# Four instead of two head tiles on the first half of the tokens at four phase borders, their low parts on GpSimd

## The chip, the cores and the metric

One core of one Trainium2 chip runs one program. The metric is the device time of one execution in microseconds (us). The engines in the texts: TensorE (PE), VectorE (DVE), ScalarE (ACT), GpSimd (POOL), SyncE (SP), and the DMA queues.

## What is computed

512 tokens of 1024 features pass through a first block of two layers (each a mixer and a feed-forward network, FFN, with layer norms after them) and a second block (a hybrid mixer and a mixture of experts). All is float32.

```python
def first_block(x, ...):
    for l in range(DEPTH):                       # DEPTH = 2
        ...
        x = layer_norm(ALPHA * x + m, ln1_g[l], ln1_b[l])
        f = conv_ffn(x, w_up[l], conv_w[l], conv_b[l], w_down[l])
        x = layer_norm(ALPHA * x + f, ln2_g[l], ln2_b[l])

def conv_ffn(x, w_up, conv_w, conv_b, w_down):
    h = x @ w_up
    hp = jnp.pad(h, ((0, 0), (CONV_W - 1, 0), (0, 0)))
    h = sum(hp[:, j:j + S] * conv_w[j] for j in range(CONV_W)) + conv_b
    u, g = jnp.split(h, 2, axis=-1)
    return (jax.nn.silu(g) * u) @ w_down

def odd_mixer(x, w_in, w_out, lq1, lk1, lq2, lk2, sub_g, rel_bias, layer):
    q, k, v = jnp.split(x @ w_in, 3, axis=-1)
    ...
    lam = (jnp.exp(jnp.sum(lq1 * lk1)) - jnp.exp(jnp.sum(lq2 * lk2)) + lam_init)
    o = diff_attention(q, k, v, lam, rel_bias)
    ...

def hybrid_mixer(h, w_in, b_in, ...):
    z = h @ w_in + b_in
    conv_a, conv_gate, q, k, v, o, i_pre, f_pre = jnp.split(z, ...)
    u = conv_a * jax.nn.sigmoid(conv_gate)
    u = causal_depthwise_conv(u, conv_w, conv_b)
    ...
```

## The kernel before

**Matmuls.** A float32 product is made of three matmuls: every operand is split into a high part (hi: a rounded copy made on ACT, the casts of L139, L280, L327) and a low part (lo: the rest, a subtraction on DVE or GpSimd, L140, L281, L329). `mm3` (L148 to L151) issues hi x hi, hi x lo and lo x hi. `fm_tile` computes 128 features for all 512 tokens (8 steps of 128 inputs, 24 matmuls of 128x512, or of 128x256 for half the tokens); `tm_tile` computes 128 tokens for 512 features.

**Weights.** `Stream` (L36 to L70) loads 232 units of 512 KB in a fixed order, two raw buffers deep, splits each into `wh` (ACT, L139) and `wl` (L140), with four buffers of each, and hands them out with `take(ahead)`, which also splits the next `ahead` units. The lo is a DVE subtraction, except for "easy" units, where GpSimd makes it: a range of late units, and the first NH units at each of the four heads in HEADS, (36, 102, 134, 200). NH is 3.

**Phase borders.** A phase ends with an output projection in `proj_ln` (L202). Its last part goes through the four blocks of 128 tokens one after the other; after each, `ln_finish` (L252) does the layer norm on DVE (L258 to L264; before the mixer another norm, L742 to L744, follows), and `to_fm` (L270) transposes the block on PE in two groups of four (L277, into `tp` banks of the tag `at`), with the hi copy on ACT (L280) and the lo on DVE (L281) into `xTh` and `xTl`. The transposes of blocks 0 and 1 are called inside `proj_ln`; those of blocks 2 and 3 are handed to the next phase as `pend`.

**The head of a phase.** At four borders (FFN of layer 0, mixer of layer 1, FFN of layer 1, mixer of the second block) `head_pair` (L175) starts the next phase with two tiles, 256 tokens first: 48 matmuls of 128x256, then `pend`, then the second 256 tokens. PSUM has eight banks: 2 of tag `mm`, 5 of `at`, 1 of `y`. The two head tiles take `at` banks. After it, tiles are 512 tokens wide in `mm` banks.

**Layer 1.** After the head, `stacks` and `lam` (L573) prepare the attention: lambda comes from a DMA on GpSimd's queue (L577, `wt<-in_lam_dram`), a DVE multiply (L579) and reduction (L581), an exponential on ACT (L582, with its table load) and two small DVE steps. `rel_table` (L549) sends the bias table `relo` to `reld` (L565) and spreads it with eight DMAs `skew<-reld` (L569), on the same queue. `qk(h)` turns a q tile and a k tile into stacks of hi and lo (`stack_q` L320, L321; `stack_k` L327 to L329), which the score matmuls (`ds`, L605) read. The order is `qk(0)`, `vproj(0)` (four value units, 96 matmuls of 128x512), `qk(1)`, `qk(2)`, `vproj(1)`.

**Mixer of the second block.** The head's two tiles are `conv_a` and `conv_gate` of the first 128 channels, used by `ag(0)` (L973 sigmoid, L976 product u). u feeds a convolution of 31 products on DVE, ACT and GpSimd (L754 to L766). `if_gates` (L801) projects the gates (24 matmuls, `gi`) and scans them on DVE and ACT (L816 to L825) into R, which PE transposes (`gt`, L830).

A scheduler sets the order of each engine's instructions from its own plan of times; the engines then run in that order and wait for one another through semaphores.

Of the kernel before, what the change touches and what calls it, by code (L numbers as in the profile page):

```python
# [75 lines left out]

class Kern:
    PRE, POST, FEW, LEAD = 2, 9, 2, 2
    YC, NH = 2, 3
    NPL, EASY, HEADS = 6, (200, 228), (36, 102, 134, 200)  # L80

    def __init__(self, tc, A, out, stop=None):
# [89 lines left out]
            if kt in self.steps:  # L172
                self.step()

    def head_pair(self, xT, pend):  # L175

        w0 = self.ws.take()
        w1 = self.ws.take()
        p0, p1 = self.ps("at"), self.ps("at")
        for p, w in ((p0, w0), (p1, w1)):  # L180
            self.fm_tile(p, w, xT, False, 0, 256)
        for f in pend:
            f()
        for p, w in ((p0, w0), (p1, w1)):
            self.fm_tile(p, w, xT, False, 256, 512)
        return p0, p1

    def rstd_(self, out, var, eps, scale=1.0):

# [472 lines left out]
    def layer1(self, xT, pend):  # L662
        nc, tc, A = self.nc, self.tc, self.A
        lam_init = 0.8 - 0.6 * math.exp(-0.3)
        first = self.head_pair(xT, pend)
        with self.pool("m1") as mp:
            self.mp = mp
            qks = self.stacks(2)
# [14 lines left out]
            def qk(h):  # L683
                for l in heads:
                    self.room(l, 1)
                if h == 0:
                    p, p2 = first
                else:
                    p = self.ps("mm")
                    self.fm_tile(p, self.ws.take(), xT)  # L690
                while h > 1 and ("scores", h - 2) not in self.ready:
                    self.step()
                self.stack_q(p, qks[h % 2], -0.125)
                if h:
                    p2 = self.ps("mm")
                    self.fm_tile(p2, self.ws.take(), xT)
                self.stack_k(p2, qks[h % 2])
                heads[h % 2].append(self.diff(h, qks[h % 2]))
                if h:
                    self.step()  # L700
# [9 lines left out]
                    self.step()  # L710

            qk(0)
            vproj(0)
            qk(1)
            qk(2)
            vproj(1)
            for h in range(3, 8):
# [7 lines left out]
            pend = self.out_proj()  # L725
# [190 lines left out]

    def mixer2(self, xT, pend):
        nc, tc, A = self.nc, self.tc, self.A
        first = self.head_pair(xT, pend)
        self.act2 = self.pool("act2", "left")  # L920
        ap = self.ap = self.act2.__enter__()
        mp = self.mp = self.open("m2")
# [38 lines left out]
        vec = self.vec  # L961

        def ag(j):
            if j == 0:
                pa, pg = first
            else:
                pa = self.ps("mm")
                self.fm_tile(pa, self.ws.take(), xT)
                self.step()
                pg = self.ps("at")  # L970
                self.fm_tile(pg, self.ws.take(), xT)
            s = mp.tile([128, 516], F32, name="sig", tag="z", bufs=1)[:, 0:512]
            nc.scalar.activation(s, pg, AF.Sigmoid, bias=vec[:, 1, j:j + 1])  # L973
            u = mp.tile([128, 544], F32, name="u31", tag="u31", bufs=3)
            nc.gpsimd.memset(u[:, 0:30], 0.0)
            nc.vector.scalar_tensor_tensor(u[:, 30:542], pa, vec[:, 0, j:j + 1], s, op0=ALU.add, op1=ALU.mult)  # L976
            convs.append(self.conv31(j, u))
            self.step()
# [603 lines left out]

    def ffn(self, l, xT, pend, finish_of):
        nc, tc = self.nc, self.tc
        first = self.head_pair(xT, pend)
        with self.pool("ffn") as fp:
            act = fp.tile([128, NP, 512], F32, name="act")
            cw = self.cw
# [8 lines left out]
                return h  # L1597

            for j in range(NP):
                if j == 0:  # L1600
                    pu, pg = first
                    u = conv(pu, j, "u")
                else:
                    pu = self.ps("mm")
                    self.fm_tile(pu, self.ws.take(), xT)
                    u = conv(pu, j, "u")
# [80 lines left out]
def layout(I):  # L1687
# [36 lines left out]
    f = fm(w)  # L1724
    q, k = f[:8], f[8:16]
    v = [list(vm(w[:, 2048:2560])), list(vm(w[:, 2560:3072]))]
    u += [q[0], k[0]] + v[0] + [q[1], k[1], q[2], k[2]] + v[1]
    for h in range(3, 8):
        u += [q[h], k[h]]
    u += list(dm(I["w_out_odd"][0]))  # L1730
# [75 lines left out]
```

## Time and profile before

| | us |
|---|---|
| median of the runs | 2063.57 |
| lowest and highest of them | 2062.98, 2067.83 |
| the profiled execution | 2058.57 |
| its span | 2056.9 |

In the profile's page PE is busy for 91% of the span, DVE for 46%, ACT for 37% and GpSimd for 16%. TensorE's granted clock is 0.959 of full speed (2.4 GHz) in the mean; where PE stood still it falls to 0.50. A row of the timeline has a start, a duration, the engine, the line of the program, the operation, what it writes and reads, and in brackets how long the engine stood idle before it and what released it. Matmuls are pipelined: the step from one start to the next is the cost of one, not its duration. The borders lie at about 287 us (FFN of layer 0), 660 (mixer of layer 1), 915 (FFN of layer 1) and 1290 (mixer of the second block).

### The profile page before, as it was taken

Reading aid. Unit: us, or ns where it says so; the run is one execution under the profiler, and the core shown is the slowest. Engines: PE = TensorE matmul, PEld = TensorE weight load, DVE = VectorE, ACT = ScalarE, POOL = GpSimd, SP = SyncE. Lnnn points to the kernel's source line nnn. Section 1 sums busy time; section 2 is a strip of 40 time slices with the busy share of each in tenths; the row PEclk is TensorE's granted clock in tenths of the full one; section 3 lists DMA queues with packets and bytes.
Section 4 is the critical chain, followed back from the end, with each engine's and each line's share of the span. In section 5 each row is a group of like instructions: output and inputs, shape, how many; then the busy total and the mean of one; then the engine's idle time right before and its main releaser. Section 6 shows DMA issues by size and latency. Waiting matters only on the chain. (4 is left out here: it accounts for less than half of the span.)

```text
span 2056.9 us, 28841 instructions
## 1 busy us (share of the span) xinstructions
PE 1867.7 (91%) x11078; PEld 1432.0 (70%) x11082; DVE 949.7 (46%) x1700; ACT 764.3 (37%) x1198; POOL 336.6 (16%) x344
## 2 busy tenths in 40 slices
PE   8999999999999999989999999799796698888881
PEld 6777878888887788878888888677575354444440
DVE  5556365545436456665454435766746011101113
ACT  6547334333322477724333323454731100000002
POOL 0001111111001100011111100545212112222212
PEclk9999999999999999999999999899797799999996
DMA  5221233332322513123323232322166999999994
GB/s 183 87 82 47 88 105 103 99 97 95 100 93 82 162 59 106 47 79 116 103 93 102 93 100 66 96 66 88 42 255 233 365 409 379 391 383 414 406 410 179
DMA packets 71527, 334.19 MB, mean 162 GB/s; under 512 B 10794, under 2 KB 11018, under 8 KB 49328
## 3 DMA queue, kind: packets, MB, share of 16 engines
q1 hardware_dynamic: 62784, 310.06, 41.3%
q0 software_dynamic: 7984, 17.48, 2.5%
q10 hardware_dynamic: 576, 4.19, 0.5%
q8 instruction: 116, 1.90, 0.4%
q14 instruction: 67, 0.55, 0.1%
HBM read 348.44 MB, written 14.18 MB: 176 GB/s over the span
## 5 line engine op out<-in xcount | busy, mean ns | idle before, releaser
L149 PE MATMUL mm<-xTh,wh 128*128 128x512 f32 x1000 | 394.8, 395 | 6.1 <-ACT xTh L1643 6.1
L150 PE MATMUL mm<-xTl,wh 128*128 128x512 f32 x1000 | 391.7, 392 | 0.5 <-DVE xTl L1644 0.5
L151 PE MATMUL mm<-xTh,wl 128*128 128x512 f32 x1000 | 392.0, 392 | 0.0
L140 DVE TENSOR_TENSOR wl<-wraw,wh 128x1024 fp32r<-128x1024 f32 x195 | 240.4, 1233 | 326.2 <-ACT wh L139 325.1
L139 ACT CAST wh<-wraw 128x1024 fp32r<-128x1024 f32 x232 | 243.6, 1050 | 343.8 <-PE mm L150 205.4
L1354 PE MATMUL mm<-ring,xt 128*32 128x256 f32 (+1 forms) x2432 | 195.0, 414 | 63.6 <-PEq L1451 29.9
L149 PEld LDWEIGHTS mm<-xTh,wh 128*128 128x128 f32 x1000 | 188.8, 189 | 46.0 <-ACT xTh L1643 6.1
L150 PEld LDWEIGHTS mm<-xTl,wh 128*128 128x128 f32 x1000 | 188.8, 189 | 39.8 <-DVE xTl L1644 1.1
L151 PEld LDWEIGHTS mm<-xTh,wl 128*128 128x128 f32 x1000 | 188.6, 189 | 39.4 <-issue 0.4
L1354 PEld LDWEIGHTS mm<-ring,xt 128*32 128x32 f32 (+1 forms) x2432 | 118.4, 126 | 136.1 <-issue 65.2
L140 POOL TENSOR_TENSOR wl<-wraw,wh 128x1024 fp32r<-128x1024 f32 x37 | 93.4, 2532 | 578.9 <-ACT wh L139 435.9
L1358 DVE TENSOR_TENSOR a<-a,mm 128x128 f32<-128x128 f32 x56 | 16.2, 289 | 318.8 <-ACT a L1357 307.8
L1611 POOL TENSOR_TENSOR act<-u,g 128x512 f32<-128x512 f32 x44 | 57.0, 1295 | 432.7 <-ACT g L1610 432.7
L1357 ACT ACTIVATE a<-mm 128x128 f32<-128x128 f32 x56 | 15.6, 278 | 263.2 <-PE mm L1354 258.7
L1373 PE MATMUL dn<-ring,aT 128*32 128x256 f32 (+1 forms) x1120 | 105.8, 425 | 0.8 <-DVE aT L1364 0.8
L140 DVE TENSOR_TENSOR jitl<-act,jith 128x512 fp32r<-128x512 f32 x44 | 30.5, 692 | 131.8 <-ACT jith L139 131.8
L149 PE MATMUL at<-wh,jith 128*128 128x512 f32 x220 | 85.8, 390 | 0.0
L151 PE MATMUL at<-wh,jitl 128*128 128x512 f32 x220 | 85.6, 389 | 0.0
L150 PE MATMUL at<-wl,jith 128*128 128x512 f32 x220 | 85.6, 389 | 0.0
L1378 POOL DMA_INDIRECT yd<-yo,yi x42 | 42.7, 1017 | 259.6 <-POOLq L1451 171.3
L139 ACT CAST jith<-act 128x512 fp32r<-128x512 f32 x44 | 27.4, 623 | 137.3 <-PE y L150 126.1
L150 PE MATMUL mm<-wl,xTh 128*128 128x512 f32 x192 | 76.2, 397 | 1.8 <-POOL wl L140 1.8
(467 smaller groups left out, 3257.0 us busy)
## 6 DMA issues: line engine op xcount, KB each, us to landing
ring<-in_wgu_dram SPq DMA_DIRECT2D x126, 1024.0 KB
wraw<-in_w_dram SPq DMA_DIRECT2D x232, 512.0 KB
ring<-in_wdn_dram SPq DMA_DIRECT2D x62, 1024.0 KB
gb<-in_ln_dram POOLq DMA_DIRECT2D x8, 512.0 KB, 6.7
yt<-yd ACTq DMA_DIRECT2D x4, 1024.0 KB
skew<-reld POOLq DMA_DIRECT2D x8, 320.0 KB, 9.5
x<-in_xT_dram SPq DMA_DIRECT2D x8, 256.0 KB
x<-in_x_dram SPq DMA_DIRECT2D x4, 512.0 KB
```

The lines of the kernel that those rows point to most:

```text
L139: nc.scalar.copy(h, src)
L140: (nc.gpsimd if spare else nc.vector).tensor_tensor(l, src, h.bitcast(F32), op=ALU.subtract)
L149: mm(out, lh, rh, start=first, stop=False)
L150: mm(out, lh, rl, start=False, stop=False)
L151: mm(out, ll, rh, start=False, stop=last)
L1354: mm(p[g * W:g * W + W, 0:256], xt[:, kt % n, kt // n, :], w[:, kt % 4, g * C + c:g * C + c + 256], start=kt == 0, stop=kt == KT - 1)
L1357: nc.scalar.activation(a, p[:, 0:128], AF.Silu)
L1358: V.tensor_tensor(a, a, p[:, 128:256], op=ALU.mult)
L1373: mm(p[g * W:g * W + W, 0:C], aTs[kt % n][:, (kt // n) * W:(kt // n) * W + W], w[:, kt, g * C:g * C + C], start=kt == 0, stop=kt == 3)
L1378: st = nc.gpsimd.indirect_dma_start(out=yv[G == 2], out_offset=bass.IndirectOffsetOnAxis(ap=ix, axis=0), in_=y, in_offset=None, bounds_che ...
L1611: nc.gpsimd.tensor_tensor(act[:, j, :], u, g, op=ALU.mult)
```

## The change

`head` takes the place of `head_pair`: four tiles, in the banks `mm`, `mm`, `at`, `at`, take four units, do their first 256 tokens (96 matmuls of 128x256), then the pending transposes, then the second 256 tokens. NH becomes 4, so GpSimd makes the low parts of all four (units 39, 105 and 137 come from DVE; unit 203 was GpSimd's). The phases take the second pair of tiles from the head too: the FFN its second u and g, layer 1 the q and k of its second head (so `qk(1)` stands ahead of `vproj(0)`, and the units are loaded in that order), the mixer the second pair of `conv_a` and `conv_gate`.

```diff
-    YC, NH = 2, 3
+    YC, NH = 2, 4
...
-    def head_pair(self, xT, pend):
-
-        w0 = self.ws.take()
-        w1 = self.ws.take()
-        p0, p1 = self.ps("at"), self.ps("at")
-        for p, w in ((p0, w0), (p1, w1)):
+    def head(self, xT, pend):
+
+        ts = [(self.ps(tag), self.ws.take(int(i < 3))) for i, tag in enumerate(("mm", "mm", "at", "at"))]
+        for p, w in ts:
             self.fm_tile(p, w, xT, False, 0, 256)
         for f in pend:
             f()
-        for p, w in ((p0, w0), (p1, w1)):
+        for p, w in ts:
             self.fm_tile(p, w, xT, False, 256, 512)
-        return p0, p1
+        return [p for p, _ in ts]
...
-                if h == 0:
-                    p, p2 = first
+                if h < 2:
+                    p, p2 = first[2 * h:2 * h + 2]
...
-                if h:
+                if h > 1:
                     p2 = self.ps("mm")
                     self.fm_tile(p2, self.ws.take(), xT)
...
             qk(0)
+            qk(1)
             vproj(0)
-            qk(1)
             qk(2)
...
-            if j == 0:
-                pa, pg = first
+            if j < 2:
+                pa, pg = first[2 * j:2 * j + 2]
...
-                if j == 0:
-                    pu, pg = first
+                if j < 2:
+                    pu, pg = first[2 * j:2 * j + 2]
...
-    u += [q[0], k[0]] + v[0] + [q[1], k[1], q[2], k[2]] + v[1]
+    u += [q[0], k[0], q[1], k[1]] + v[0] + [q[2], k[2]] + v[1]
```

Line numbers beyond L184 are two lower in the changed kernel (L277 becomes L275).

PE at the first FFN's border, from the last matmuls on the first token half over the transposes (`tp`) of blocks 2 and 3 to the second half. Before:

```order
L150 MATMUL at<-xTl,wh 128x256
L151 MATMUL at<-xTh,wl 128x256
L277 MATMUL tp<-ident,x 128x128 x12
L149 MATMUL at<-xTh,wh 128x256 x2
L149 MATMUL mm<-xTh,wh 128x512 x2
L150 MATMUL at<-xTl,wh 128x256
```

And now:

```order
L151 MATMUL at<-xTh,wl 128x256
L275 MATMUL tp<-ident,x 128x128 x16
L149 MATMUL mm<-xTh,wh 128x256 x2
L149 MATMUL at<-xTh,wh 128x256 x2
L150 MATMUL mm<-xTl,wh 128x256
L151 MATMUL mm<-xTh,wl 128x256
```

Four of the 16 transposes stood ahead of the first halves before; now all stand between the halves, and the two 512-wide matmuls that followed them are gone.

DVE at the start of layer 1's mixer, from the last lo of the tokens (L281, then L279) over lambda's steps (`wt`, `lams`) to the stacks `q` and `k`. Before:

```order
L281 TENSOR_TENSOR xTl<-tp,xTh 128x4x128 x3
L140 TENSOR_TENSOR wl<-wraw,wh 128x1024
L321 SCALAR_TENSOR_TENSOR q_4788<-at,q_4788 64x512
L140 TENSOR_TENSOR wl<-wraw,wh 128x1024
L321 SCALAR_TENSOR_TENSOR q_4791<-at,q_4791 64x512
L579 TENSOR_TENSOR wt<-wt 128x128
L673 TENSOR_SCALAR lams<-lams 128x1
L329 TENSOR_TENSOR k_4790<-at,k_4789 64x512
```

And now:

```order
L279 TENSOR_TENSOR xTl<-tp,xTh 128x4x128 x4
L577 TENSOR_TENSOR wt<-wt 128x128
L579 TENSOR_REDUCE lams<-wt 128x2
L671 TENSOR_SCALAR lams<-lams 128x1
L581 TENSOR_TENSOR lams<-lams 128x1
L582 TENSOR_SCALAR lams<-lams 128x1
L319 SCALAR_TENSOR_TENSOR q_4940<-mm,q_4940 64x512
L140 TENSOR_TENSOR wl<-wraw,wh 128x1024
L319 SCALAR_TENSOR_TENSOR q_4943<-mm,q_4943 64x512
L327 TENSOR_TENSOR k_4942<-mm,k_4941 64x512
```

Lambda's five steps moved ahead of both q stacks and of the value units' low parts.

GpSimd at the same border, where the low parts of the head's units stand ahead of the DMAs. Before:

```order
L1611 TENSOR_TENSOR act<-u,g 128x512 x22
L140 TENSOR_TENSOR wl<-wraw,wh 128x1024 x3
L565 DMA reld<-relo 8x640
L569 DMA skew<-reld 128x640 x8
L313 MEMSET k_4790 64x512
```

And now:

```order
L1609 TENSOR_TENSOR act<-u,g 128x512 x22
L140 TENSOR_TENSOR wl<-wraw,wh 128x1024 x4
L563 DMA reld<-relo 8x640
L567 DMA skew<-reld 128x640 x8
L311 MEMSET k_4942 64x512
```

The fourth subtraction stands ahead of `reld`, the skew DMAs and lambda's DMA behind them.

## Rows read from the trace of the kernel before

**Rows 1.** The page: busy time (share) xinstructions; GpSimd's low parts, xcount | busy, mean ns.
```profile
PE 1867.7 (91%) x11078; PEld 1432.0 (70%) x11082; DVE 949.7 (46%) x1700; ACT 764.3 (37%) x1198; POOL 336.6 (16%) x344
...
L140 POOL TENSOR_TENSOR wl<-wraw,wh 128x1024 fp32r<-128x1024 f32 x37 | 93.4, 2532 | 578.9 <-ACT wh L139 435.9
```

**Rows 2.** Timeline of PE, first FFN's border: start, us, engine, line, operation [idle before].
```profile
283.73 0.39 PE L150 MATMUL y<-wl,acth 128*128 128x512 f32 x1
...
286.67 0.40 PE L151 MATMUL y<-wh,actl 128*128 128x512 f32 x1
...
292.82 0.58 PE L150 MATMUL at<-xTl,wh 128*128 128x256 f32 x1 [1.13 <-DVE xTl L281]
...
301.00 1.47 PE L277 MATMUL tp<-ident,x 128*128 128x128 f32 x12
...
303.60 0.39 PE L150 MATMUL at<-xTl,wh 128*128 128x256 f32 x1
303.82 0.28 PE L151 MATMUL at<-xTh,wl 128*128 128x256 f32 x1
...
307.78 0.28 PE L149 MATMUL at<-xTh,wh 128*128 128x256 f32 x1
```

**Rows 3.** Timeline of DVE, first FFN's border.
```profile
292.09 0.68 DVE L281 TENSOR_TENSOR xTl<-tp,xTh 128x512 fp32r<-128x512 f32 x1
...
297.00 1.28 DVE L264 SCALAR_TENSOR_TENSOR x<-x,mv,gb 128x1024 f32<-128x1024 f32 x1
```

**Rows 4.** Windows, first FFN's border: us, busy of each engine, PEclk, DMA share, GB/s.
```profile
296.00:298.00 2.00, 2.00 (x11) 2.00 (x11) 2.00 (x2) 0.00 (x0) 0.00 (x0) 0.50 0.93 281
```

**Rows 5.** Timeline of PE, second FFN's border.
```profile
927.30 1.47 PE L277 MATMUL tp<-ident,x 128*128 128x128 f32 x12
...
929.90 0.38 PE L150 MATMUL at<-xTl,wh 128*128 128x256 f32 x1
```

**Rows 6.** Timeline of PE, the mixer's border.
```profile
1301.42 1.47 PE L277 MATMUL tp<-ident,hn 128*128 128x128 f32 x12
1303.42 0.66 PE L277 MATMUL tp<-ident,hn 128*128 128x128 f32 x4 [0.53 <-DVE xTl L281]
...
1304.62 0.39 PE L150 MATMUL at<-xTl,wh 128*128 128x256 f32 x1
```

**Rows 7.** Timeline of GpSimd, layer 1's border.
```profile
663.12 2.37 POOL L140 TENSOR_TENSOR wl<-wraw,wh 128x1024 fp32r<-128x1024 f32 x1 [1.34 <-ACT wh L139]
666.88 0.53 POOL L565 DMA_DIRECT2D reld<-relo  x1 [1.39 <-ACT relo L563]
...
676.24 0.58 POOL L577 DMA_DIRECT2D wt<-in_lam_dram  x1 [0.29 <-DMA skew<-reld]
```

**Rows 8.** Timeline of DVE, layer 1's border.
```profile
663.20 3.37 DVE L263 SCALAR_TENSOR_TENSOR x<-x,mv,gb 128x1024 f32<-128x1024 f32 x1
...
682.15 0.69 DVE L321 SCALAR_TENSOR_TENSOR q<-at,q 64x512 fp32r<-64x512 f32 x1
686.59 0.29 DVE L579 TENSOR_TENSOR wt<-wt 128x128 f32<-128x128 f32 x1 [3.75 <-DMA wt<-in_lam_dram]
```

**Rows 9.** Timeline of PE, layer 1, end of the head and the second score.
```profile
679.69 0.40 PE L149 MATMUL mm<-wh,xTh 128*128 128x512 f32 x1
...
688.16 0.76 PE L605 MATMUL ds<-k,q 128*128 128x512 f32 x1 [3.55 <-DVE k L329]
...
691.27 0.39 PE L149 MATMUL mm<-wh,xTh 128*128 128x512 f32 x1
```

**Rows 10.** Timeline of ACT, layer 1's border.
```profile
665.29 1.04 ACT L139 CAST wh<-wraw 128x1024 fp32r<-128x1024 f32 x1 [1.29 <-DMA wraw<-in_w_dram]
...
679.82 1.05 ACT L139 CAST wh<-wraw 128x1024 fp32r<-128x1024 f32 x1 [1.22 <-issue]
680.89 0.60 ACT L320 ACTIVATE q<-at 64x512 fp32r<-64x512 f32 x1
681.51 0.58 ACT L327 CAST k<-at 64x512 fp32r<-64x512 f32 x1
```

**Rows 11.** Timeline of PE, the mixer: the transposes of R.
```profile
1333.23 0.23 PE L830 MATMUL gt<-ident,R 4*128 4x4 f32 x1 [5.23 <-DVE R L823]
```

More of the change, by code (lines that the diff above doesn't have):

```diff
@@ L664, in layer1 @@
         lam_init = 0.8 - 0.6 * math.exp(-0.3)
-        first = self.head_pair(xT, pend)
+        first = self.head(xT, pend)
         with self.pool("m1") as mp:
@@ L918, in mixer2 @@
         nc, tc, A = self.nc, self.tc, self.A
-        first = self.head_pair(xT, pend)
+        first = self.head(xT, pend)
         self.act2 = self.pool("act2", "left")
@@ L1584, in ffn @@
         nc, tc = self.nc, self.tc
-        first = self.head_pair(xT, pend)
+        first = self.head(xT, pend)
         with self.pool("ffn") as fp:
```

## The prediction

> **What bounds the kernel now.** I read the page first: TensorE (PE) is busy for 91% of the span, and GpSimd makes 37 low parts of weights at 2.53 us each [rows 1]. So the time falls only where PE stands still or repeats work, and rises with every matmul that is added. I then read the PE timeline at the four phase borders that the change touches (into the first FFN, into layer 1, into the second FFN, into the mixer), since elsewhere the order of PE's instructions is the same in both kernels or only shifted; then DVE, ACT, GpSimd and the waits in the same stretches. I use "hi" and "lo" for the two parts of a split number.
>
> At the first FFN's border [rows 2] the last projection matmul starts at 286.67. The first head matmul that needs xTl starts at 292.82, after the lo of block 1 at 292.09 [rows 3]. PE then runs the 48 first halves, until 301.00, without a stop. The point for this change is what happens there: the last layer norm step of block 3 ended on DVE at 297.00 + 1.28 = 298.3 [rows 3], so the transposes of blocks 2 and 3 start at 301.00 with their input lying ready for 2.7 us. **PE does not wait for the second half of the tokens in the kernel before.** What is left is a gap of 2.6 us for 12 transposes and their evictions, until the first lo matmul of the second half at 303.60. The second FFN has the same picture: transposes at 927.30, lo matmul at 929.90 [rows 5]. The mixer's border has it with 16 transposes, the last four behind an `at` buffer (0.53 us of wait): 1301.42 to 1304.62, 3.2 us [rows 6]. Before the first xTl matmul the chain is projection, layer norm, transpose, lo, and nothing of the change is in it: on DVE the order up to the lo of block 1 is unchanged.
>
> The first stretch of head matmuls runs at half clock, 1.2 GHz, in the kernel before (granted 0.50 from 296 to 298) [rows 4]. A column costs the same there whichever tile it belongs to, so I count the half clock as equal.
>
> **The change part by part.**
>
> *More narrow matmuls.* From the rows, 33 steps of 256 columns take 307.78 - 303.82 = 3.96 us, 0.12 each, and 13 steps of 512 columns 286.67 - 283.73 = 2.94 us, 0.2265 each [rows 2]. At each border 96 more matmuls of 256 take the place of 48 of 512: 96 x 0.12 - 48 x 0.2265 = 11.52 - 10.87 = +0.65 us.
>
> *Transposes in one block.* All 16 now stand together behind the 96 first halves, with two `at` banks held by the head, which is the mixer's pattern before: 3.2 us instead of 2.6. The two FFN borders pay +0.6 each, with the 0.65 **+1.25 each, +2.5 for both**. The bounds: 0.65 if the four extra transposes find a hole, 1.9 if the last four wait twice as long.
>
> *Fourth low part on GpSimd.* Three units move from DVE to GpSimd. At the FFN borders that delays nothing that PE waits for: tile 3 of the head is used some 10 us after its hi part exists, and block 3's layer norm has over 10 us more than before. At the layer-1 border GpSimd also issues the DMAs of the bias table and of lambda. In the kernel before it finishes its third low part at 663.12 + 2.37 = 665.5, waits for `relo`, issues `reld` at 666.88, then eight skew DMAs, and lambda's at 676.24 [rows 7]. The fourth low part stands ahead of `reld`; its cast ends about 666.3 (in the kernel before that cast starts at 665.29 and takes 1.04 [rows 10]), so `reld` goes about 2 us later, at 668.9, and everything behind it on that queue too. Lambda's data, used at 686.59 before [rows 8], comes at about 688.6.
>
> What the traces show of GpSimd beside DVE: the layer norm step at 663.20 took 3.37 us [rows 8] under a GpSimd subtraction that began at 663.12 [rows 7], against 1.28 for the same kind of step alone [rows 3]. The Trainium skill, "SBUF — State Buffer", section "Who interferes with whom", says that a DVE instruction with two SBUF inputs and a GpSimd instruction that reads SBUF lock each other out through a shared port pair. By that rule, which the 3.37 us agree with, the change is worse than its instruction count: the fourth subtraction meets block 3's last step and ends about 1.2 us later, and the sum below would be +5.2 instead of +4.0.
>
> *Layer 1, the second head's stacks.* PE: the second halves ended at 679.6 before [rows 9]. Now the first halves end 48 x 0.12 = 5.8 us later, the second halves have 46 more matmuls, 5.5, and the gap is 3.2 instead of 3.0: the head ends at about 679.7 + 5.8 + 5.5 + 0.2 = 691.2. Work for work that is +0.65 and +1.1, the latter because five 512-wide matmuls of the value projection used to lie in the gap. What follows is the larger matter. In DVE's order lambda's multiply, which waits for the DMA, now stands ahead of the first q stack, and on ACT lambda's exponential ahead of the first q copy. Behind these wait the q and k stacks of both heads, the low parts of the value weights, and through both PE, whose next four instructions are scores. Before, only the k lo waited: PE lost 3.55 us at 688.16, and then took 691.27 - 688.16 = 3.11 us for seven matmuls that cost 1.59 at full clock, 1.5 lost: 5.05 together [rows 9]. Now the fourth score needs, after lambda's arrival, the multiply (0.29), reduction and exponential (0.9 with the multiply, an estimate from its size), on ACT two q copies (0.60), four k copies (0.58) and two weight casts (1.05), 5.6 us [rows 10], and the last k lo on DVE, 0.69 like the q lo [rows 8]; with hand-overs 7.4 us. That is 688.6 + 7.4 = 696.0, against a PE free at 691.2 with three scores (0.7 us) to do: 4.1 us idle, and I take the same 1.5 for the clock. **Border: 0.65 + 1.1 - 5.05 + 4.1 + 1.5 = +2.3.** Bounds: lambda in time and no stall, 1.75 - 5.05 = -3.3; lambda three us later than I have it, +8 (below).
>
> *Mixer border.* +0.65 for the narrow matmuls; the gap is the same 3.2. Later PE waits 5.23 us for R at 1333.23 [rows 11], with 48 wide matmuls (10.9 us) between the gate projection and it, before and after. The chain behind the gate projection loses at least a weight cast on ACT (1.05 [rows 10]) that stood between its two activations, and has its conv products further ahead; I count 1.5 us, between 0 and the whole 5.23. **Border: -0.85.**
>
> **Sum:** 2.5 + 2.3 - 0.85 = **+3.95 us**. The profiled execution took 2058.57, 5 us under the median of the runs, 2063.57; I take the difference as valid for both: 2062.5 and **2067.5 us**.
>
> **The rivals.**
>
> *The layer-1 wait disappears.* If lambda lands before the q stacks can start (about 683, when tile 0 is finished), the chain of 7.4 us ends before 691.2 and the old stall is gone. Border -3.3, sum 2.5 - 3.3 - 0.85 = -1.65, and with the whole gate wait saved at the mixer -5.4: 2058 to 2062. Against it: lambda's data came at 686.59 from a queue that now starts later.
>
> *The layer-1 wait grows, and the kernel is slower by over 0.3%* (0.3%, 6.2 us here, is about what a measurement can tell from no change). One mechanism: lambda's DMA waits behind eight skew transfers that run beside more weight loads. With its arrival at 691.6 the fourth score comes at 699.0: idle 7.1, clock 2.5, and the value projection's first low parts, queued behind lambda on DVE too, hold PE 1.5 more. Border +7.8, and the sum is +6.2 where the arrival is about 2 us later than mine; at 691.6 with nothing gained at the mixer, +11: 2074.5.
>
> *The borders fill as the change's shape suggests.* If the longer first half covered the gaps before the second half at all four borders, it would save the idle part of each, some 2.5 us, 10 us together less 2.6 for narrow matmuls, and with the layer-1 wait gone 13: about 2051. Against it: block 3 is ready at 298.3 and asked for at 301.0; the gap is transposes and their evictions, and the change puts no matmul among them.
>
> **How the numbers follow.** Chances: my forecast, with the layer-1 border between -1 and +5: 0.62. Wait gone: 0.17. Wait grown: 0.17. Borders filled: 0.04. The first case reaches beyond +6.2 in part (the borders at their upper bounds, or a wait at R that stays whole): 0.12 of it. So slower by over 0.3%: 0.17 + 0.12 = 0.29. Faster by over 0.3% (below 2057.4): the filled borders and the tail of the gone wait, 0.07. Within: 0.64. The range leaves out the filled borders and the last part of the grown wait: 2059 to 2075.
>
> **What would show it.** In the changed profile: 96 matmuls of 256 before the 16 transposes, starting at about 292.8 as before; the transposes at about 312 in the first border, and 3.2 us to the first lo matmul; `reld` issued about 2 us later; DVE waiting at lambda's multiply until 688 to 689 and PE idle some 4 us near 692 to 696, at half clock after it; the wait at R under 5.23. I am wrong if lambda's wait is under 2 us, if the first xTl matmul starts earlier (the layer norm chain would then be shorter than I read it), or if the second halves wait for a weight's low part.

## The result, and the profile after

The changed kernel takes 2075.81 us (median, 2075.31 to 2077.34), the kernel before 2063.78 (2062.98 to 2067.83): a ratio of 1.0058 with a 95% interval of 1.0047 to 1.0069, so 12.0 us (9.7 to 14.2) slower. The forecast was 2067.5 in a range of 2059 to 2075. The profiled execution took 2075.51 us, its span is 2073.8.

The page after (busy time and share; GpSimd's low parts, count | busy, mean ns) answers to [rows 1]: 196 more matmul records, three more low parts on GpSimd, shares as before.

```profile
PE 1878.6 (91%) x11274; PEld 1447.4 (70%) x11274; DVE 957.8 (46%) x1697; ACT 758.6 (37%) x1194; POOL 344.3 (17%) x347
...
L140 POOL TENSOR_TENSOR wl<-wraw,wh 128x1024 fp32r<-128x1024 f32 x40 | 101.7, 2548 | 574.6 <-ACT wh L139 431.9
```

Where the time went is told by stages. A stage runs from the first transpose of a phase's projection (the first `tp` row at each border in the timelines of PE) to the next one's; the mixer's ends at the router's first transpose, after which PE's order is the same in all kernels.

| stage, us | before | after | difference |
|---|---|---|---|
| first FFN (280.6 to 651.6) | 371.1 | 372.3 | +1.2 |
| layer 1's mixer (to 908.1) | 256.5 | 259.4 | +2.9 |
| second FFN (to 1278.0) | 369.9 | 372.2 | +2.3 |
| mixer of the second block (to 1545.1) | 267.1 | 271.0 | +3.9 |
| experts, to the end of the span | 511.8 | 518.9 | +7.1 |

The last line needs care: the profiled execution of the kernel before lies 5 us under the median of its runs, that of the changed kernel at it. If those 5 us lie in this stage, which no run shows, about 2 of the 7 stand for the kernels.

**The first FFN's border after** (timeline of PE) answers to [rows 2].

```profile
286.33 1.04 PE L275 MATMUL tp<-ident,x 128*128 128x128 f32 x8
...
290.77 0.41 PE L149 MATMUL at<-xTh,wh 128*128 128x256 f32 x1 [2.66 <-ACT wh L139]
292.25 0.58 PE L150 MATMUL mm<-xTl,wh 128*128 128x256 f32 x1 [1.07 <-DVE xTl L279]
...
305.94 1.47 PE L275 MATMUL tp<-ident,x 128*128 128x128 f32 x12
307.94 0.66 PE L275 MATMUL tp<-ident,x 128*128 128x128 f32 x4 [0.53 <-DVE xTl L279]
...
309.13 0.39 PE L150 MATMUL mm<-xTl,wh 128*128 128x256 f32 x1
```

The first xTl matmul comes 5.9 us after the transposes of block 1 (292.25 - 286.33), as before; the 96 first halves run through; then 309.13 - 305.94 = 3.2 us of transposes and evictions. That is the forecast picture, but for the place of the transposes: they start at 305.94, not at about 312.

**Layer 1 after**: timelines of GpSimd, DVE and PE, which answer to [rows 7 to 9].

```profile
669.66 0.53 POOL L563 DMA_DIRECT2D reld<-relo  x1
673.78 4.21 POOL L567 DMA_DIRECT2D skew<-reld  x8 [3.59 <-DMA reld<-relo]
...
679.90 0.58 POOL L575 DMA_DIRECT2D wt<-in_lam_dram  x1
```
```profile
691.70 0.29 DVE L577 TENSOR_TENSOR wt<-wt 128x128 f32<-128x128 f32 x1 [9.41 <-DMA wt<-in_lam_dram]
```
```profile
695.83 0.49 PE L603 MATMUL ds<-k,q 128*128 128x512 f32 x1 [3.05 <-ACT k L326]
696.81 0.47 PE L603 MATMUL ds<-k,q 128*128 128x512 f32 x1 [0.49 <-DVE k L327]
698.10 1.64 PE L603 MATMUL ds<-k,q 128*128 128x512 f32 x2 [0.82 <-ACT k L326]
```

`reld` goes 2.1 us later against the start of the stage, lambda's DMA 3.0, and its data comes at 691.70, 3 us later than I had it; DVE stands still for 9.41 us ahead of the stacks, and PE waits 4.4 us at the scores, with half clock (granted 0.50) from 697.2 to 704.0, 6.8 us of it; 3.4 us before (687.8 to 691.2).

**The mixer after.** This is the part that I had wrong, so both kernels are shown. First DVE's and ACT's gate chain before (u is the first product; S and R belong to the gates; DVE takes up the gate projection at 1317.15), with GpSimd's low part beside it, then the chain after.

```profile
1311.36 0.74 DVE L976 SCALAR_TENSOR_TENSOR u<-at,vec,sig 128x512 f32<-128x512 f32 x1
...
1317.15 0.74 DVE L816 TENSOR_SCALAR S<-gi,bif 36x512 f32<-36x512 f32 x1 [1.02 <-PE gi L151]
...
1329.02 1.39 DVE L822 TENSOR_TENSOR_SCAN R<-ones,S 4x512 f32<-4x512 f32 x1
...
1331.10 1.99 DVE L823 TENSOR_TENSOR R<-S,R 4x512 f32<-4x512 f32 x1
```
```profile
1323.48 0.63 ACT L818 ACTIVATE S<-S 4x512 f32<-4x512 f32 x1
```
```profile
1329.29 3.26 POOL L140 TENSOR_TENSOR wl<-wraw,wh 128x1024 fp32r<-128x1024 f32 x1
```

After:

```profile
1322.79 0.74 DVE L974 SCALAR_TENSOR_TENSOR u<-mm,vec,sig 128x512 f32<-128x512 f32 x1
...
1332.92 0.74 DVE L814 TENSOR_SCALAR S<-gi,bif 36x512 f32<-36x512 f32 x1 [0.96 <-PE gi L151]
...
1345.02 3.03 DVE L820 TENSOR_TENSOR_SCAN R<-ones,S 4x512 f32<-4x512 f32 x1
...
1348.75 1.99 DVE L821 TENSOR_TENSOR R<-S,R 4x512 f32<-4x512 f32 x1
```
```profile
1340.91 0.63 ACT L816 ACTIVATE S<-S 4x512 f32<-4x512 f32 x1
```

GpSimd after, in the same stretch:

```profile
1327.27 2.42 POOL L140 TENSOR_TENSOR wl<-wraw,wh 128x1024 fp32r<-128x1024 f32 x1
1329.64 1.29 POOL L762 TENSOR_TENSOR c31b<-c31b,c31t 128x512 f32<-128x512 f32 x1
1330.88 0.09 POOL L985 MEMSET z<- 128x3 f32 x1
1330.94 2.39 POOL L140 TENSOR_TENSOR wl<-wraw,wh 128x1024 fp32r<-128x1024 f32 x1
...
1344.63 5.57 POOL L140 TENSOR_TENSOR wl<-wraw,wh 128x1024 fp32r<-128x1024 f32 x2 [5.79 <-ACT wh L139]
```

And PE, which answers to [rows 11], first the other seven transposes of R before, then after; behind them windows (us, busy of PE, PEld, DVE, ACT, POOL, PEclk, DMA share, GB/s) of ten us after the wait, and of the whole stage before and after:

```profile
1336.80 0.59 PE L830 MATMUL gt<-ident,R 4*128 4x4 f32 x7
```
```profile
1350.79 0.27 PE L828 MATMUL gt<-ident,R 4*128 4x4 f32 x1 [6.99 <-DVE R L821]
...
1353.82 0.91 PE L828 MATMUL gt<-ident,R 4*128 4x4 f32 x7 [1.61 <-DVE R L823]
```
```profile
1350.00:1360.00 10.00, 7.59 (x22) 5.17 (x23) 9.49 (x14) 3.31 (x5) 0.29 (x2) 0.53 0.17 54
```
```profile
1277.95:1545.08 267.13, 236.25 (x1058) 183.70 (x1060) 179.45 (x335) 139.97 (x205) 105.15 (x85) 0.92 0.31 109
```
```profile
1283.89:1554.92 271.03, 239.69 (x1110) 187.93 (x1108) 180.90 (x335) 137.63 (x203) 104.56 (x85) 0.91 0.31 108
```

From the gate projection to the gates' exponential: 1340.91 - 1332.92 = 8.0 us, 6.3 before. The exponential stands on ACT behind copies for the convolution, each of which waits for a product on GpSimd, and between those products stand low parts of 2.4 us. The scan took 3.03 us instead of 1.39, while GpSimd made two low parts. Before, too, a low part ran beside the scan, but the scan had started 0.27 us ahead of it (1329.02 and 1329.29), and there it was the low part that took 3.26 us instead of 2.4; after, GpSimd started first (1344.63 and 1345.02). So the first wait for R is 6.99 instead of 5.23. A second wait of 1.61 is new: before, eight wide matmuls stood between the first transpose of R and the other seven, now two. At half clock after it the steps cost 3.3 us more than at full clock (1.7 before).

The waits for R are not the whole of it. Over the stage PE stood still for 267.13 - 236.25 = 30.9 us before and 271.03 - 239.69 = 31.3 us after: other waits shrank by about as much as those for R grew. In these two profiles nearly all of the 3.9 us lies in PE's steps: 0.65 of it by the narrow matmuls (the forecast's figure), the rest mostly at half clock. What several profiles say stands below.

### The profile page after: what moved, and what is told of

Read it like the earlier page. It is cut to its first block, busy times and chain, and to the rows that moved or that the text cites. A ratio compares the mean times of both kernels' runs of the same rounds, so it can differ in the third digit from the quotient of the medians.

```text
span 2073.8 us, 29239 instructions
## 1 busy us (share of the span) xinstructions
PE 1878.6 (91%) x11274; PEld 1447.4 (70%) x11274; DVE 957.8 (46%) x1697; ACT 758.6 (37%) x1194; POOL 344.3 (17%) x347
## 5 line engine op out<-in xcount | busy, mean ns | idle before, releaser
L149 PE MATMUL mm<-xTh,wh 128*128 128x512 f32 (+1 forms) x1072 | 411.4, 385 | 7.1 <-ACT xTh L1641 6.2
L150 PE MATMUL mm<-xTl,wh 128*128 128x512 f32 (+1 forms) x1072 | 410.6, 383 | 3.2 <-DVE xTl L279 2.4
L151 PE MATMUL mm<-xTh,wl 128*128 128x512 f32 (+1 forms) x1072 | 409.8, 382 | 0.0
L1352 PE MATMUL mm<-ring,xt 128*32 128x256 f32 (+1 forms) x2432 | 198.5, 420 | 74.4 <-PEq L1449 32.6
L149 PEld LDWEIGHTS mm<-xTh,wh 128*128 128x128 f32 x1072 | 205.8, 193 | 45.6 <-ACT xTh L1641 6.2
L150 PEld LDWEIGHTS mm<-xTl,wh 128*128 128x128 f32 x1072 | 207.1, 193 | 42.3 <-DVE xTl L279 4.3
L151 PEld LDWEIGHTS mm<-xTh,wl 128*128 128x128 f32 x1072 | 207.0, 193 | 37.5 <-issue 0.4
L140 POOL TENSOR_TENSOR wl<-wraw,wh 128x1024 fp32r<-128x1024 f32 x40 | 101.7, 2548 | 574.6 <-ACT wh L139 431.9
L140 DVE TENSOR_TENSOR jitl<-act,jith 128x512 fp32r<-128x512 f32 x44 | 32.6, 741 | 126.5 <-ACT jith L139 126.2
L149 PE MATMUL mm<-wh,xTh 128*128 128x512 f32 x192 | 78.3, 408 | 0.0
## 6 DMA issues: line engine op xcount, KB each, us to landing
x<-in_xT_dram SPq DMA_DIRECT2D x8, 256.0 KB
```

Of the source, the lines that this page charges most:

```text
L140: (nc.gpsimd if spare else nc.vector).tensor_tensor(l, src, h.bitcast(F32), op=ALU.subtract)
L149: mm(out, lh, rh, start=first, stop=False)
L150: mm(out, lh, rl, start=False, stop=False)
L151: mm(out, ll, rh, start=False, stop=last)
L1352: mm(p[g * W:g * W + W, 0:256], xt[:, kt % n, kt // n, :], w[:, kt % 4, g * C + c:g * C + c + 256], start=kt == 0, stop=kt == KT - 1)
```

## The experiments

Ratios are against runs of the kernel before on the same chip, with the 95% interval; 0.1% is 2.1 us. In these intervals, mostly 2 to 3 us to either side, a border's part of 1 or 2 us can't be seen, so the stages of the profiles stand beside them.

**One part at a time.** First, four tiles with DVE making the fourth low part:

```diff
-    YC, NH = 2, 4
+    YC, NH = 2, 3
```

> The changed kernel with NH back at 3: four tiles, but DVE makes the fourth low part at the borders. Theory A (the cost lies in what the four tiles do at each border: narrow matmuls and the longer transpose block at the FFNs, the stacks behind lambda in layer 1, the gate chain in the mixer): still 8 to 11 us slower than the kernel before; at layer 1 lambda lands some 2 us earlier, so the wait there shrinks from 4.4 to about 2.5 us. Theory B (the fourth low part on GpSimd, by the delayed DMAs and by blocking DVE, is the cost): at most 3 us slower than before.

Measured 2071.65 us, 1.0047 (1.0029 to 1.0065): theory A. Layer 1's stage fell to 255.9 us, level with the kernel before (256.5), and the scores' waits to 2.7 us, as expected. That the fourth low part is the whole loss there is not shown: the run with the second pair taken up late (below) kept it, and its layer 1 took 256.0 us. The mixer, where that unit was GpSimd's anyway, stayed slow (273.6).

The opposite, two tiles with the fourth low part on GpSimd:

```diff
-    YC, NH = 2, 3
+    YC, NH = 2, 4
```

> The kernel before with NH = 4 and nothing else: two head tiles, the fourth unit's low part on GpSimd. Theory A: 0 to 3 us slower than before, all of it at layer 1, where lambda's data lands some 2 us later and the wait before the second score grows from 3.55 to about 5.5 us. Theory B: 8 us or more slower.

Measured 2066.13 us, 1.0015 (1.0003 to 1.0028), as theory A had it, and all of it in layer 1: its stage took 261.6 us, 5.1 more than before, where the runs give 3.1 (0.6 to 5.8) in all. The second score waited 4.94 us for the k lo instead of 3.55.

Then the old head in one phase, first in the mixer:

```diff
     def mixer2(self, xT, pend):
...
-        first = self.head(xT, pend)
+        first = self.head(xT, pend, 2)
...
-            if j < 2:
+            if j < 1:
```

> The changed kernel with the old head of two tiles in the mixer of the second block alone. Theory A: the mixer's part goes, 4.3 us by the two traces, so 7 to 8.5 us slower than the kernel before; the wait for R is 5.2 us again instead of 7.0 + 1.6. Rival C (the extra time at the mixer is only shifted and given back later, or comes from the later start of the expert weights): 10 to 12 us slower, as the changed kernel.

Measured 2062.56 us, 0.9998 (0.9985 to 1.0011). Both expectations missed: with two tiles in the mixer alone the runs show no loss at all. The mixer's stage is 264.3 us, the wait for R 5.2 us. Rival C falls. Theory A expected the other three borders to cost 7 us or more; why they cost nothing here is not explained by the stages (below).

In layer 1 alone, with the old order of units and of `qk(1)`, and unit 105 back on DVE:

```diff
-        first = self.head(xT, pend)
+        first = self.head(xT, pend, 2)
...
             qk(0)
-            qk(1)
             vproj(0)
+            qk(1)
```

> The changed kernel with the old head of two tiles (and three low parts on GpSimd, and the old order of units) in layer 1 alone. Theory A: layer 1's part goes, 3 to 4 us by the two traces, so 8 to 9 us slower than the kernel before; the wait at the second score is 3.5 us again and the half clock behind it lasts about 3 us, not 8. Rival D (the wait behind lambda was given back within the layer): 11 to 12 us slower.

Measured 2068.13 us, 1.0026 (1.0015 to 1.0037): faster than expected. Layer 1's stage was 257.6 us, 1.8 under the changed kernel's, but not by the mechanism expected: the second score waited 6.65 us, not 3.5, with lambda's data at 689.71. The mixer stayed at 270.5.

At the FFN borders alone (two tiles in layer 1 and the mixer, the two edits above together):

> The changed kernel with the old head of two tiles in layer 1 and in the mixer, so four tiles at the two FFN borders alone. By the prediction's sum +2.5 us, by the stages of the profiles +1.1 and +2.1: 2 to 4 us slower than the kernel before. Rival L (what the FFN borders lose is taken up by a later wait, as for the kernel with two tiles in the mixer alone, which came out level with the kernel before): within 1 us of it.

Measured 2068.53 us, 1.0023 (1.0011 to 1.0036): slower by 4.7 us, 2.3 at the lower end, so rival L falls. The FFN stages were 371.3 and 372.0. The mixer's stage, with two tiles and a wait for R of 5.21 us, took 270.0 us in this profile.

**The runs do not add up.** With four tiles at the FFN borders throughout, the mixer's head of four costs 0.60% (12.4 us) beside four tiles in layer 1 (1.0058 against 0.9998), but 0.03% (0.6 us) beside two (1.0026 against 1.0023). The four intervals do not allow for that: by their ends the first is 7 us or more, the second at most 5.3. The kernels with ratios 0.9998 and 1.0023 have the same instructions in the same order on every engine from the second FFN's border on; yet their mixers took 264.3 and 270.0 us in the profiles, their expert phases 510.3 and 517.9. So stages that an edit does not touch differ by several us from kernel to kernel. Why is open, and the price of a single border is known no better than that.

**Layer 1's wait.** Lambda's DMA on another queue, in the changed kernel:

```diff
-        nc.gpsimd.dma_start(l, bass.AP(tensor=a.tensor, ...))
+        nc.sync.dma_start(l, bass.AP(tensor=a.tensor, ...))
```

> The changed kernel with lambda's DMA issued on SP's queue instead of behind the skew DMAs on GpSimd's. Theory A (in layer 1 the stacks wait for lambda): lambda is there before the first stack, PE's 4.4 us of waits at the first scores fall to under 1 us and the half clock behind them goes, so 5 to 8 us faster than the changed kernel, 4 to 7 us slower than the kernel before. Rival E (the wait there is ACT's and DVE's own work on eight stacks and the weights): at most 2 us faster than the changed kernel.

Measured 2075.93 us, 1.0063 (1.004 to 1.0086): nothing gained, and theory A seemed to fall. The timeline of DVE says why. Lambda is done early; then another small DMA, still on GpSimd's queue, takes its place, the gain of the norm, and the stacks stand behind that:

```profile
673.46 0.29 DVE L577 TENSOR_TENSOR wt<-wt 128x128 f32<-128x128 f32 x1 [3.35 <-DMA wt<-in_lam_dram]
...
688.34 0.15 DVE L671 TENSOR_SCALAR lams<-lams 128x1 f32<-128x1 f32 x1 [7.53 <-DMA lams<-in_subg_dram]
```

The same edit in the kernel before:

> The kernel before with lambda's DMA on SP's queue, nothing else. Theory A: the wait of 3.55 us at the second score goes and with it the half clock (1.5 us): 4 to 5 us faster than the kernel before. Rival E: within 2 us of it.

Measured 2059.26 us, 0.9986 (0.9971 to 1.0001): 2.9 us faster, with no change just inside the interval as well as the 4 us of theory A. Layer 1's stage took 253.5 us, 3.0 less, and the second score still waited 1.91 us. So both were moved, first in the changed kernel:

```diff
-            nc.gpsimd.dma_start(self.subg, A["subg"])
+            nc.sync.dma_start(self.subg, A["subg"])
```

> The changed kernel with both small DMAs of layer 1 that stood behind the skew DMAs, lambda's and the sub-norm gain's, on SP's queue. With lambda's alone moved, DVE stood 7.5 us before the gain's step instead, and the q and k stacks behind it. Theory A2 (the stacks wait for whichever of these two DMAs comes last): DVE no longer waits there, the four first scores follow the head with under 1.5 us of waits instead of 4.4, and the stage from layer 1's border to the second FFN's falls from 258 or 259 us to about 253; 4 to 6 us faster than the changed kernel. Rival E (ACT's own chain of copies is as long): at most 2 us faster.

Measured 2072.54 us, 1.0052 (1.0037 to 1.0067), stage 256.5 us. DVE's last wait for a DMA ends at 673.13, long before the stacks, but the third score waits 3.17 us for ACT's copies of k, and the kernel is only 1.2 us under the changed one by the ratios. Theory A2 names the first wait rightly, and behind it stands rival E's, ACT's own stack copies and weight casts. In the kernel before:

> The kernel before with both small DMAs on SP's queue. Theory A2: the waits before the first two scores (3.9 us) go altogether with the half clock behind them: 4 to 6 us faster than the kernel before, and 0 to 2 us faster than with lambda's alone. Rival E: as with lambda's alone, where 1.9 us of wait on the k lo were left.

Measured 2059.43 us, 0.9987 (0.9977 to 0.9998): 2.7 us faster (0.4 to 4.7), level with the run that moved lambda's alone. The stage took 252.0 us, 4.5 less than before, and the first two scores waited 1.4 us in all instead of 2.3 with lambda's alone. So the profile speaks for A2; the runs do not tell A2 from rival E.

**The gap at the borders.** Pending transposes asked for among the first halves of the four tiles:

```diff
-        for p, w in ts:
+        for p, w in ts[:2]:
             self.fm_tile(p, w, xT, False, 0, 256)
-        for f in pend:
-            f()
+        pend[0]()
+        for p, w in ts[2:3]:
+            self.fm_tile(p, w, xT, False, 0, 256)
+        pend[1]()
+        for p, w in ts[3:]:
+            self.fm_tile(p, w, xT, False, 0, 256)
```

> The changed kernel with the pending transposes asked for inside the first halves: block 2's behind the second tile, block 3's behind the third. Theory A (the gap before the second half is transposes and evictions with no matmul among them): the gap of 3.2 us goes at all four borders and eight of the transposes cost about 0.9 us each time: 6 to 9 us faster than the changed kernel, 3 to 6 us slower than the kernel before. Rival H (the evictions are late wherever the transposes stand, since DVE and ACT are busy with the layer norm): at most 3 us faster than the changed kernel.

Measured 2070.53 us, 1.0033 (1.0016 to 1.005): 5.2 us under the changed kernel by the ratios, between theory A's 6 to 9 and rival H's 3. The timeline of PE at the second FFN's border:

```profile
915.87 1.86 PE L279 MATMUL tp<-ident,x 128*128 128x128 f32 x8 [2.48 <-DVE x L266]
926.74 1.03 PE L279 MATMUL tp<-ident,x 128*128 128x128 f32 x8
927.53 0.36 PE L149 MATMUL at<-xTh,wh 128*128 128x256 f32 x1
```

Block 2's eight transposes lie in a wait that was there anyway, block 3's cost 927.53 - 926.74 = 0.8 us among the first halves, and no gap is left. That stage takes 368.7 us, 3.5 less than the changed kernel's and 1.2 less than before; theory A is right there. The mixer did not gain (274.1).

**What holds the mixer.** Units 204 to 207, the four after the head, to DVE:

```diff
-            self.ws.easy = set(range(*self.EASY)) | {...}
+            self.ws.easy = (set(range(*self.EASY)) | {...}) - {204, 205, 206, 207}
```

> The changed kernel with the low parts of units 204 to 207, the four after the mixer's head, on DVE instead of GpSimd. Theory F (in the mixer the gates' exponential on ACT waits behind conv products that GpSimd delays by three low parts of 2.4 us): no low part stands between the first five products on GpSimd, the exponential comes 3 to 5 us earlier, and PE's waits for R fall from 8.6 to 4 us or less; 3 to 5 us faster than the changed kernel. Rival G (the chain is DVE's own, with four more subtractions of 1.23 us ahead of the gates): waits for R of 8 us or more, no faster than the changed kernel.

Measured 2079.17 us, 1.0075 (1.0048 to 1.0101). The mechanism is there and the gain is not: the exponential came 5.4 us after the gate projection instead of 8.0 and the waits for R fell to 6.3 (theory F had 4 or less), but later waits for GpSimd's low parts rose from 1.0 to 4.2 us, and the stage took 273.7.

Units 208 and 209 instead (the pair beside the scan), in the same line:

> The changed kernel with the low parts of units 208 and 209 on DVE instead of GpSimd. In the changed kernel the scan of R on DVE took 3.03 us (1.39 before) while GpSimd made these two low parts. Theory F2 (the scan is blocked by GpSimd's subtraction): the scan takes 1.4 us again; with the one low part of 1.2 us that DVE now has ahead of R, the first wait for R falls from 7.0 to 6.0 to 6.6 us; the stage from the mixer's border to the router stays at 269 to 272 us. Rival M (the scan is slow for another reason): 3 us again, and the wait grows.

The timeline of DVE:

```profile
1343.68 1.21 DVE L820 TENSOR_TENSOR_SCAN R<-ones,S 4x512 f32<-4x512 f32 x1
...
1346.07 0.67 DVE L821 TENSOR_TENSOR R<-S,R 4x512 f32<-4x512 f32 x1
```

3.03 and 1.99 us became 1.21 and 0.67 with GpSimd standing still: F2 is shown, the waits for R fell to 5.9 us. Measured 2077.88 us, 1.0076 (1.0058 to 1.0094), stage 270.5, with 4.2 us of waits for GpSimd's low parts here too: again nothing came of it. All six units:

> The changed kernel with units 204 to 209 on DVE, so that no low part of GpSimd stands before the exponential or beside the scan. With 204 to 207 alone the first wait for R fell from 7.0 to about 4.4 us, but later waits for GpSimd's low parts grew by 3 us. Theory F + F2: exponential early and scan of 1.4 us, waits for R of 4 to 5 us in all; if nothing else takes their place the stage falls to 267 us, otherwise (the low parts only move to another queue) it stays at 270 us or more.

Measured 2073.74 us, 1.0059 (1.0042 to 1.0075), waits for R 3.7 us, stage 274.1 us, in the slowest of its four runs: no gain, though the waits for R are below those of the kernel before. The second pair taken up later:

```diff
         heads.append(self.if_gates(xT))
-        ag(1)
         masks()
         qk(0)
+        ag(1)
```

> The changed kernel with the mixer's second gated pair (its product and convolution) taken up after the first q and k tiles, as late as in the kernel before; the four tiles of the head stay. Theory F (the gate chain is late because the second pair's steps and four low parts on GpSimd stand ahead of the exponential and the scan): the second pair's product and copy leave the chain, four conv products on DVE take their place, three low parts on GpSimd stay ahead of it: wait for R of 6 to 8.5 us, stage of 269 to 272 us. Theory N (it is the second pair alone): wait for R of 5.2 us and a stage of 266 us as with two tiles.

Measured 2073.1 us, 1.0061 (1.004 to 1.0083), wait for R 6.6 us, stage 270.0: theory N falls. Taking away one wait after the other did not help; the old head did. What the head of four does in any case, and what these runs keep, is to start the mixer's other engines later: DVE's first product u stood 33.4 us after the border before (1311.36 - 1278.0) and stands 38.9 us after it now (1322.79 - 1283.9), since the first pair's second halves wait for 48 more first halves. The third product stands at 109.4 and 115.1: about the same, carried through the stage. That this is the cause, rather than the sum of the waits, is inferred from these runs and was not tried alone; against it stands the kernel with four tiles at the FFN borders alone, whose u came at 33.3 us and whose mixer took 270.0 us.

**Versions put together from what paid.** Four tiles at three borders with transposes among them, two in the mixer, NH = 3, both small DMAs on SP:

> A version put together from the parts that paid: four tiles at the two FFN borders and in layer 1 with the pending transposes among the first halves, DVE making the fourth low part (NH = 3), both small DMAs of layer 1 on SP's queue, and the old head of two tiles in the mixer. From the stages of the profiles: -0.5 and -1.2 us at the FFN borders, -4 to -6 at layer 1, 0 in the mixer against the kernel before: 5 to 8 us faster than it. Rival K (the parts do not add up, as the waits behind layer 1's border only move): within 3 us of it.

Measured 2050.4 us, 0.9943 (0.9927 to 0.9958): 11.8 us faster, more than the 5 to 8 expected. Two tiles everywhere, with the same DMAs and block 2's transposes between the two tiles:

```diff
-        for p, w in ((p0, w0), (p1, w1)):
-            self.fm_tile(p, w, xT, False, 0, 256)
-        for f in pend:
-            f()
+        self.fm_tile(p0, w0, xT, False, 0, 256)
+        pend[0]()
+        self.fm_tile(p1, w1, xT, False, 0, 256)
+        pend[1]()
```

> The kernel before (two head tiles everywhere, NH = 3) with both small DMAs on SP's queue and block 2's transposes asked for between the two tiles of the head. It tells whether the four tiles are worth anything in the version that was fastest (0.57% faster than the kernel before, with four tiles at three borders). Theory P (the gain there is that no transposes are left in a gap, for which two tiles are enough): as fast as that version, 10 us or more faster than the kernel before. Theory Q (two tiles end before block 3's transposes can lie among them): 4 to 7 us faster than the kernel before, as with the DMAs alone.

Measured 2056.94 us, 0.9977 (0.9964 to 0.999): 4.7 us faster, theory Q's figure. At the mixer this place of the transposes brought u 3 us later (36.6) and a wait for R of 5.75 us; its stage, 267.6 us, lies within what two tiles take anyway. It was left out there, and the version of four ran beside it:

> Two head tiles at all four borders, both small DMAs of layer 1 on SP's queue, block 2's transposes between the two tiles at the FFN borders and in layer 1, and the mixer's border as in the kernel before (in the run with the early transposes at the mixer too, the wait for R there was 5.8 instead of 5.2 us and the stage 267.6 us). Theory P (the place of the transposes and of the DMAs is the whole gain of the fastest version): within 3 us of that version, which runs beside it. Theory Q (the four tiles at three borders add to it): 5 us or more slower than that version.

> The fastest version once more, on the same chip as the run with two tiles: 0.4 to 0.7% faster than the kernel before by its first run. Theory P: level with the two-tile version beside it. Theory Q: 5 us or more faster than it.

Measured 2055.59 us, 0.9968 (0.9956 to 0.9979), and 2052.41 us, 0.9953 (0.994 to 0.9966). The two lie 3.2 us apart, between theory P's 3 and theory Q's 5, and the intervals overlap; up to the router the stages add to 1255.2 and 1254.1 us. Most of the gain lies in the place of the transposes and of two small DMAs; whether the four tiles add 3 us to it is not settled. Both beat the kernel before.

The stages of the profiles by group, mean and range:

| stage, us | two tiles | four tiles | difference |
|---|---|---|---|
| first FFN | 370.4 (369.8 to 371.1, 4 kernels) | 371.6 (371.1 to 372.6, 11) | +1.2 |
| layer 1 (two: NH 3; four: NH 4) | 256.5 (255.3 to 257.6, 3) | 258.0 (256.0 to 259.4, 6) | +1.5 |
| second FFN | 370.5 (369.9 to 371.1, 4) | 372.2 (371.3 to 372.6, 11) | +1.7 |
| mixer | 265.6 (263.2 to 270.0, 9) | 271.6 (270.5 to 273.6, 5) | +6.0 |

Kernels with other edits in a stage are left out of its line; each profile is one execution, and two of the nine in the mixer's line are the same kernel on two chips (263.7 and 263.2). In layer 1 the ranges overlap. The sum is +10.4 us, against 12.0 (9.7 to 14.2) by the runs. Of the mixer's +6.0, PE stands still for 2.7 us (32.6 against 30.0 in the mean) and is busy for 3.4 us more: 0.65 by the narrow matmuls, the rest mostly at half clock.

## Why the prediction was wrong

- *PE does not wait for the second half of the tokens:* right. Nothing was saved at any border by the longer first half, the gap is 3.2 us, and with the transposes moved into the halves it was gone.
- *Narrow matmuls and one block of transposes, +1.25 at each FFN border:* right, +1.2 and +1.7 by the groups. The rest at the second is half clock: its first halves lost 2.9 us there with four tiles in the changed kernel's profile, 1.4 before. Where half clock lasts equally long at a border, the profiles of the two groups differ by 1.3 to 1.5 us at either FFN. The transposes at about 312 were a slip: my own terms, 301.0 + 5.8, give 306.8, and they came at 305.94.
- *Fourth low part on GpSimd, layer 1's queue and stacks, +2.3:* the border's sum was near (+1.5 by the groups, +2.9 in the first two profiles), partly by luck. Lambda came 3 us later than I had it, since the wait for `reld` grew too (3.59 us for 2.35); the scores' waits of 4.4 us were as forecast (4.1) only because the head ended 1.6 us later as well (695.83 - 3.05 = 692.8 for 691.2); the half clock behind them lasted 6.8 us, and I had taken the cost of the 3.4 of before. That lambda was the one DMA on which it hung was wrong: the norm's gain behind it would have held the stacks as long.
- *The mixer, -0.85:* this is the step that failed. I took the gate chain to lose a cast, and bounded the wait for R between all of 5.23 us and nothing saved. The cast did go (the chain's two activations on ACT start 1.9 us apart, 3.0 before), but the chain as a whole grew. No row excluded a loss, and in the changed kernel GpSimd splits units 204 to 209 while the gates run; I had priced GpSimd's low parts in layer 1 only. The waits became 6.99 + 1.61, with 1.6 us more lost at half clock. This much is shown in every profile: PE waits 5.19 to 5.23 us for R in the nine of the mixer's line with two tiles, 8.6 to 9.0 in the five with four. The stage is 6.0 us slower by the groups: 6.9 of the 8 us between forecast and result. That these 6.0 are all due to the head is less sure: the ranges all but touch (270.0 and 270.5), the runs give 12.4 or 0.6 us by what stands in layer 1, and no run that kept the head of four and shortened the waits for R brought the stage below 270.
- *The rivals:* the wait in layer 1 neither went nor grew by much. None of the three was the mixer. The measured 2075.81 lies near the second one's 2074.5, but not by its mechanism.
- *GpSimd and DVE:* the Trainium skill, "SBUF — State Buffer", section "Who interferes with whom", holds that a DVE instruction with two SBUF inputs and a GpSimd instruction that reads SBUF lock each other out. Rows agree in both places: 3.37 us for 1.28 at a layer norm step, which nobody waited for, and 3.03 for 1.21 at the scan, which PE waited for. In these rows the one that began second was held up: the scan that began 0.27 us ahead took 1.39 us, and the GpSimd subtraction 3.26. I had weighed the rule at the first place and not looked for the second.

## What to carry to other kernels

Work taken ahead of a border's second half delays everything that the first tiles feed: here the first product for DVE came 5.5 us later, and in the mixer, whose other engines run chains of their own, PE's waits for one such chain grew by 3.4 us where I had forecast a gain. Before a first half is made longer, look whether the second half is late at all; here it lay ready for 2.7 us, and the gap was transposes, which were better placed among the matmuls that were there. When one wait is taken away, look at what stands next on the same queue: behind lambda's DMA stood another, and behind both ACT's copies. And differences of a few us between stages of single profiles need more than one pair: the same instructions in the same order took 264.3 and 270.0 us.

## What the runs showed of the hardware

- In nine profiles with the same two tiles the mixer's stage took 263.2 to 270.0 us. In the shortest and the longest, below, every engine has the same instructions in the same order, and PE stands still equally long (263.16 - 232.40 = 30.8 us and 269.99 - 239.04 = 31.0). It is busy 6.6 us longer in the second, where the mean granted clock is 0.91 instead of 0.94. The same stalls of PE do not have a fixed price in half clock (1.2 GHz).

```profile
1270.47:1533.63 263.16, 232.40 (x1061) 181.40 (x1060) 178.75 (x335) 139.92 (x205) 105.71 (x85) 0.94 0.31 110
```
```profile
1278.79:1548.78 269.99, 239.04 (x1061) 186.14 (x1060) 178.64 (x335) 139.97 (x205) 105.50 (x85) 0.91 0.31 106
```

- The expert phase, with the same order of PE in all kernels, took 509.9 to 517.9 us in the profiles with two tiles in the mixer and 515.2 to 529.2 with four. What the runs leave for it, 12.0 less 10.4, is under 2 us, and nothing at all lies within the interval. What moves it was not found; it stays open.
- A subtraction of 4 x 512 values on DVE took 0.67 us alone and 1.99 beside a GpSimd subtraction that had begun before it, in the kernel before too.
